# Gate weights split anew in every block of a streaming conformer layer, instead of stored split

## The chip, the cores and the metric

The kernel runs on one core of a Trainium2 chip. The metric is the time of one execution on the device, in microseconds (us). The engines are TensorE (PE in the profile; its weight loads are PEld), VectorE (DVE), ScalarE (ACT), GpSimd (POOL) and SyncE (SP), which here only issues transfers between HBM and SBUF. Each engine works through its own instructions in order and waits on semaphores for the others.

## The reference

One layer of a hybrid streaming encoder over 2048 prompt tokens and 64 sample tokens, with 1024 channels. The parts that matter:

```
h = rms_norm(x) * (1 + sc1) + sh1
z = h @ w_in                      # 1024 x 4608
glu_a, glu_b, q, k, v, g_conv, g_attn = split(z)   # 512 x5, 1024 x2
u = glu_a * sigmoid(glu_b)
conv_out = silu(layer_norm(depthwise31(u))) @ w_conv_out
attn_out = band_attention(q, k, v) @ w_attn_out    # 8 heads of 64
merged = sigmoid(g_conv) * conv_out + sigmoid(g_attn) * attn_out
x = x + gt1 * (merged @ w_o)
x = x + gt2 * swiglu_ffn(rms_norm(x) ...)
```

All of it is float32. The two gates are 2048 of the 4608 columns of `w_in`; their weights are what the change is about.

## The kernel before, in words

**Precision.** TensorE multiplies in fp32r. To keep float32 accuracy, every operand is split in two: `hi` is the value copied to fp32r, `lo` is the value minus `hi`. A product is three matmuls, hi by hi, hi by lo and lo by hi (`mm3`). So each weight slab exists as a pair `whi`, `wlo`: ScalarE makes `whi` by a copy, and `wlo` is a subtraction on VectorE or GpSimd.

**Two parts.** Part one (to about 1192 us) works through four blocks of tokens (576, 512, 512, 512). In each block come the stages q, glu0, k, glu1, v, glu2, glu3 and g, the gates. The gates of a block are 16 columns of 128 channels; their weights are 16 slabs of 128 partitions x 1024 numbers (512 KB), two for a pair of columns. Beside these matmuls of TensorE run, as lanes that a planner interleaves: the attention heads, the depthwise convolution (31 taps for each of four channel groups, on VectorE, `y<-u,wd,y`), its layer norm (`conv_norm`: sums on GpSimd in tile `s`, means by matmul in `pm`), the norm of the next block's tokens (`norm_tile`: load `x_t`, transpose into `pt`), and the conditioning products. Part one leaves the convolution's result in `c_d`, attention's in `o_d` and the gates in `g_d`, all in HBM. Part two merges them with the gates (`merge`, from `cin` and `tg`), and does the output projection and the feed-forward.

**Weights.** The class `Weights` holds a list of keys in order of use. At its making, it decides which occurrence of a key is loaded raw (an `item`: staged in `wst`, three buffers, then split) and which is taken from a split copy in HBM: a key that `kept` names and that comes again is loaded raw once; `split` then writes `whi` and `wlo` to HBM (`w_d...`), and later occurrences load the pair from there, ready for use. A key ("in", column, h) of three elements is a gate slab; a key ("in", column) of two is a slab of the GLU. `whi` and `wlo` each have five buffers. In `split`, `on_dve` says where the low part is computed.

**What sets the order.** `Stream` and `Lane` form a planner: each instruction that is written adds an estimate to its engine's load, and a lane takes its next step when the step's due time is reached by TensorE's load and when the named engines are not too far ahead of it. Transfers are issued at due times in the same way. So an estimate added to ScalarE or GpSimd moves what is written after it. The result is written to each engine's queue, and the queue is in order.

**End of part one.** The convolution's norm of block 3 ends with four groups `ln`, each split into `part_h` (ScalarE) and `part_l` and stored to `c_d`; the last heads end with the same kind of pair, stored to `o_d`. There are two buffers of each. Then part two's pools take the place of part one's, and the first tiles there wait for the last users of that space.

Of the kernel before, what the change touches and what calls it, by code (L numbers as in the profile page):

```python
# [263 lines left out]
class Weights:  # L264
# [5 lines left out]
    def __init__(self, engines, pool, dram, stream, keys, source, staging, held, kept):  # L270
        self.stream = stream
        self.sync, self.act, self.dve, self.gps = engines
        self.pool, self.dram, self.keys, self.source = pool, dram, keys, source

        self.staging, self.held, self.reach = staging, held, 0
        self.sum_pool, self.sum_d, self.sums, self.hold, self.landed = None, None, {}, 0, {}
        self.behind = nullcontext

        self.room, self.leaving = {"wst": 1, "wup": 0, "wfo": 0}, {"wst": 0, "wup": 0, "wfo": 0}
        times, raws = {}, {}  # L280
        self.items, self.users, self.need, self.first, self.stored, self.spread = [], [], {}, set(), {}, set()

        def item(key):
            self.items.append(key)
            self.users.append(0)
            return len(self.items) - 1

        for i, key in enumerate(keys):
            n = times[key] = times.get(key, 0) + 1
            if key[0] == "up" and n == 1:  # L290
                self.first.add(i)
                cs = [c for f, op in key[1:] for c in self.columns_of(f, op)]
                for c in cs:
                    if c not in raws:
                        raws[c] = item(("fi", c))
                self.need[i] = sorted({raws[c] for c in cs})
                for f, op in key[1:]:
                    for c in self.parts_of(f, op):
                        self.users[raws[c]] += 1
            elif key[0] == "dn":  # L300
                fs = [key[:3], (*key[:2], key[2] + 1)]
                for f in fs:
                    if f not in raws:
                        raws[f] = item(("fo", f[2]))
                self.need[i] = [raws[f] for f in fs]
                for op in key[3:]:
                    for e in self.rows_of(op):
                        self.users[raws[fs[e]]] += 1
            elif n == 1 or not kept(key) or n == 2 and key[:2] == ("qkv", 0):
                self.need[i] = [item(key)]  # L310
                self.users[self.need[i][0]] += 1
                if key[0] == "fo" and key[1] in last_rows(0) and n == 1:
                    self.spread.add(self.need[i][0])
        self.raws = raws
# [136 lines left out]
    def split(self):  # L451
        i = len(self.ready)
        key = self.keys[i]
        its = self.need.get(i, ())
        if key[0] == "dn":
            shape = [P, len(key) - 3, 512]
        elif i in self.first:
            shape = [P, 4 * len(key) - 4, P]
        else:
            shape = list(self.loaded[its[0]][0].shape) if its else self.stored[key][1]  # L460
        hi = self.pool.tile(shape, F32R, tag="whi", name="whi", bufs=self.held)
        lo = self.pool.tile(shape, F32R, tag="wlo", name="wlo", bufs=self.held)
        self.ready.append((hi, lo))
        if not its:
            for t, d in zip((hi, lo), self.stored[key][0]):
                self.sync.dma_start(t.bitcast(F32), d)
            return
        turn = {"wo": key[1], "fi": key[1] // P if key[0] == "fi" else 0}.get(key[0], 0)

        passing = key[:2] == ("qkv", 0) and i < 4  # L470
        on_dve = key[0] == "in" or key[0] == "qkv" and (passing or key[1]) or turn % 2
        if key[0] == "dn":
            parts = [(slice(j, j + 1), self.second(key, op)) for j, op in enumerate(key[3:])]
            self.stream.after("act", "pool")
        elif i in self.first:
            parts = [(slice(4 * j, 4 * j + 4), self.operand(f, op)) for j, (f, op) in enumerate(key[1:])]
            self.stream.after("act", "pool")
        else:
            n = 4 if key[0] == "fi" else shape[1]
            parts = [(slice(j, j + n), self.loaded[its[0]][0][:, j : j + n]) for j in range(0, shape[1], n)]  # L480
        for c, src in parts:

            late = key[0] in ("up", "fo") and self.stream.load["pool"] - self.stream.load["pe"] > POOL_BEHIND
            e, name = (self.dve, "dve") if on_dve or late else (self.gps, "pool")
            self.act.activation(hi[:, c], src, AF.Copy)
            self.stream.after(name, "act")
            e.tensor_tensor(lo[:, c], src, hi[:, c].bitcast(F32), ALU.subtract)
        if i in self.first:
            its = [self.raws[c] for f, op in key[1:] if op[0] == "a" for c in self.parts_of(f, op)]
        if key[0] == "dn":  # L490
            its = [self.raws[*key[:2], key[2] + int(op[1]) - 1] for op in key[3:] if op[0] == "b"]
        for j in its:
            self.drop(j, name)
        if key[0] == "dn" and key[3] == "b11":
            self.sum_second(key)

        def then():
            if key in self.again and key not in self.stored and not passing:
                ds = [self.dram.tile(shape, F32, name="w_d" + "_".join(map(str, key)) + "_" + part) for part in "hl"]
                for t, d in zip((hi, lo), ds):  # L500
                    self.sync.dma_start(d, t.bitcast(F32))
                self.stored[key] = ds, shape
            self.presum()

        self.stream.at(self.stream.when(name), then, True)
# [67 lines left out]


DOWN_OPERANDS = (("b11", "b21"), ("t3", "t2"), ("t1", "t4"), ("b22",))


def mod_order():
# [33 lines left out]
def streaming_layer(ctx: ExitStack, tc: tile.TileContext, I, O):  # L612
    nc = tc.nc
# [973 lines left out]
    M.fill()  # L1587
    next(vectors_)
    xs = first_rows()
    W = Weights((nc.sync, act, dve, gps), wpool, dram, stream, list(weight_order()), source, 3, 5, lambda key: key[0] in KEPT)  # L1590
    first_block(xs)
    norm_lane.add(cached_kv())
    mods = mod_steps()
# [661 lines left out]
```

## Time and profile before

| | us |
|---|---|
| runs | 2988.55, 2989.11, 2995.56 |
| median | 2989.11 |
| span of the profiled execution | 2982.2 |
| part one, start to first `cin` matmul | 1192.3 |
| TensorE busy | 2906.6 (97%) |
| VectorE busy | 2047.4 (69%) |
| ScalarE busy | 1363.6 (46%) |
| GpSimd busy | 1165.8 (39%) |

The profiled execution gives only its span; the runs' times also have what lies around it, so the two stand side by side, 6.9 us apart for the median.

Rows of the profile read: engine, operation, output<-inputs by the program's names, shape, count | busy us, mean ns of one | idle time of the engine just before them, and what ended most of it. A row of waits reads: engine and output, the releaser, then us in total, times, longest. A row of the timeline reads: start, duration, engine, line, operation, and in brackets the idle time before it with its releaser. Nearly all compute has line L102, a helper; tiles tell the operations apart. A window row lists each engine's busy us in that stretch with its count, then TensorE's granted clock, the DMA engines' busy share and GB/s.

### The profile page before, as it was taken

Reading aid. Unit: us, or ns where it says so; the run is one execution under the profiler, and the core shown is the slowest. Engines: PE = TensorE matmul, PEld = TensorE weight load, DVE = VectorE, ACT = ScalarE, POOL = GpSimd, SP = SyncE. Lnnn points to the kernel's source line nnn. Section 1 sums busy time; section 2 is a strip of 40 time slices with the busy share of each in tenths; the row PEclk is TensorE's granted clock in tenths of the full one; section 3 lists DMA queues with packets and bytes.
Section 4 is the critical chain, followed back from the end, with each engine's and each line's share of the span. In section 5 each row is a group of like instructions: output and inputs, shape, how many; then the busy total and the mean of one; then the engine's idle time right before and its main releaser. Section 6 shows DMA issues by size and latency. Waiting matters only on the chain. (4 is left out here: it accounts for less than half of the span.)

```text
span 2982.2 us, 44930 instructions
## 1 busy us (share of the span) xinstructions
PE 2906.6 (97%) x16241; PEld 2588.0 (87%) x16241; DVE 2047.4 (69%) x3628; ACT 1363.6 (46%) x2459; POOL 1165.8 (39%) x752
## 2 busy tenths in 40 slices
PE   7999899999999999989999999999999999999999
PEld 4899777787888888878989899999999999999998
DVE  5897687667857885477677755676666557566666
ACT  3345643662456257464443335544444345444442
POOL 0201310111011102444666443365766742465767
PEclk9999999999999999999999999999999999999999
DMA  8989889888997888885444786423333975333333
GB/s 296 304 282 306 264 286 312 279 256 276 308 283 221 281 256 277 265 284 167 139 147 149 233 268 222 135 89 113 114 106 116 308 244 184 98 96 114 114 104 126
DMA packets 467724, 628.06 MB, mean 211 GB/s; under 512 B 36276, under 2 KB 314664, under 8 KB 467501
## 3 DMA queue, kind: packets, MB, share of 16 engines
q1 hardware_dynamic: 453456, 605.58, 62.8%
q10 hardware_dynamic: 14045, 19.60, 1.9%
q8 instruction: 128, 2.10, 0.3%
q14 instruction: 95, 0.78, 0.1%
HBM read 476.53 MB, written 148.54 MB: 210 GB/s over the span
## 5 line engine op out<-in xcount | busy, mean ns | idle before, releaser
L102 PE MATMUL ps<-t,whi 128*128 128x384 f32 (+1 forms) x2112 | 502.7, 322 | 9.5 <-ACT t L102 4.9
L102 POOL TENSOR_TENSOR wlo<-wst,whi 128x1024 fp32r<-128x1024 f32 (+1 forms) x160 | 365.1, 2292 | 254.1 <-ACT whi L102 231.9
L102 ACT ACTIVATE whi<-wst 128x1024 fp32r<-128x1024 f32 (+1 forms) x264 | 257.4, 977 | 324.8 <-PE ps L102 118.5
L102 PE MATMUL ps<-b,whi 128*128 128x384 f32 (+1 forms) x1584 | 381.3, 326 | 6.1 <-DVE early L102 3.4
L102 PEld LDWEIGHTS ps<-t,whi 128*128 128x128 f32 x2112 | 367.6, 188 | 17.2 <-ACT t L102 5.1
L102 DVE SCALAR_TENSOR_TENSOR y<-u,wd,y 128x512 f32<-128x512 f32 (+1 forms) x480 | 369.1, 773 | 6.4
L102 PE MATMUL ps<-hh,whi 128*128 128x512 f32 (+2 forms) x992 | 361.3, 364 | 0.0
L102 DVE TENSOR_TENSOR acc<-acc,pd 128x512 f32<-128x512 f32 (+1 forms) x482 | 322.5, 685 | 54.9 <-PE pd L102 52.4
L102 PE MATMUL ps<-hl,whi 128*128 128x512 f32 (+2 forms) x992 | 345.2, 348 | 0.0
L102 PE MATMUL ps<-hh,wlo 128*128 128x512 f32 (+2 forms) x992 | 344.9, 348 | 0.0
L102 PE MATMUL ps<-t,wlo 128*128 128x384 f32 (+1 forms) x1056 | 339.3, 321 | 1.0 <-POOL wlo L102 0.7
L102 PE MATMUL pd<-whi,hid 128*128 128x512 f32 (+1 forms) x956 | 307.2, 391 | 0.2 <-DVE hid L102 0.2
L102 PEld LDWEIGHTS ps<-b,whi 128*128 128x128 f32 x1584 | 278.6, 189 | 12.4 <-DVE early L102 4.2
L102 POOL TENSOR_TENSOR r<-t,mhalf 128x1 f32<-128x1 f32 (+3 forms) x68 | 83.7, 1232 | 456.4 <-DVE t L102 451.3
L102 PE MATMUL ps<-b,wlo 128*128 128x384 f32 (+1 forms) x792 | 256.9, 325 | 0.0
L102 ACT ACTIVATE pr<-pr,sm 128x640 f32<-128x640 f32 (+3 forms) x272 | 200.2, 747 | 109.7 <-DVE sm L102 107.1
L102 PEld LDWEIGHTS pd<-whi,hid 128*128 128x128 f32 (+1 forms) x956 | 174.6, 183 | 42.4 <-ACT hid L102 0.7
L102 PEld LDWEIGHTS ps<-hh,wlo 128*128 128x128 f32 x992 | 186.6, 188 | 21.7
L102 PEld LDWEIGHTS ps<-hh,whi 128*128 128x128 f32 x992 | 187.2, 189 | 18.5 <-issue 1.6
L102 PEld LDWEIGHTS ps<-hl,whi 128*128 128x128 f32 x992 | 187.3, 189 | 15.5 <-issue 1.4
L102 PEld LDWEIGHTS ps<-t,wlo 128*128 128x128 f32 x1056 | 198.2, 188 | 2.6 <-POOL wlo L102 1.3
L102 POOL TENSOR_TENSOR wlo<-ws,whi 128x512 fp32r<-128x512 f32 x96 | 125.2, 1325 | 173.7 <-ACT whi L102 170.8
(227 smaller groups left out, 6307.0 us busy)
## 6 DMA issues: line engine op xcount, KB each, us to landing
whi<-w_din_h SPq DMA_DIRECT2D x72, 512.0 KB, 6.6
wlo<-w_din_l SPq DMA_DIRECT2D x72, 512.0 KB, 8.2
wst<-sum_d SPq DMA_DIRECT2D x132, 256.0 KB, 2.8
wfo<-in_w_ffn_out SPq DMA_DIRECT2D x64, 512.0 KB, 3.3
wmod<-in_w_ada SPq DMA_DIRECT2D x46, 512.0 KB, 6.2
sum_d<-ws SPq DMA_DIRECT2D x88, 256.0 KB, 2.4
wst<-in_w_ffn_in SPq DMA_DIRECT2D x84, 256.0 KB, 3.1
wst<-in_w_in SPq DMA_DIRECT2D x40, 512.0 KB, 9.1
```

The lines of the kernel that those rows point to most:

```text
L102: self.last = f(*args, **kw)
```

## The change

Gate slabs are taken out of `kept`. They are no longer written split; each block loads them raw into `wst` and splits them. The first occurrence has its low part on VectorE as before, every later one (set `anew`) on GpSimd.

```
--- before.py
+++ after.py
@@ -279,6 +279,7 @@
         self.room, self.leaving = {"wst": 1, "wup": 0, "wfo": 0}, {"wst": 0, "wup": 0, "wfo": 0}
         times, raws = {}, {}
         self.items, self.users, self.need, self.first, self.stored, self.spread = [], [], {}, set(), {}, set()
+        self.anew = set()
 
         def item(key):
             self.items.append(key)
@@ -287,6 +288,8 @@
 
         for i, key in enumerate(keys):
             n = times[key] = times.get(key, 0) + 1
+            if n > 1 and gate_slab(key):
+                self.anew.add(i)
             if key[0] == "up" and n == 1:
                 self.first.add(i)
                 cs = [c for f, op in key[1:] for c in self.columns_of(f, op)]
@@ -468,7 +471,7 @@
         turn = {"wo": key[1], "fi": key[1] // P if key[0] == "fi" else 0}.get(key[0], 0)
 
         passing = key[:2] == ("qkv", 0) and i < 4
-        on_dve = key[0] == "in" or key[0] == "qkv" and (passing or key[1]) or turn % 2
+        on_dve = key[0] == "in" and i not in self.anew or key[0] == "qkv" and (passing or key[1]) or turn % 2
         if key[0] == "dn":
             parts = [(slice(j, j + 1), self.second(key, op)) for j, op in enumerate(key[3:])]
             self.stream.after("act", "pool")
@@ -573,6 +576,11 @@
 
 
 DOWN_OPERANDS = (("b11", "b21"), ("t3", "t2"), ("t1", "t4"), ("b22",))
+
+
+def gate_slab(key):
+
+    return key[0] == "in" and len(key) == 3
 
 
 def mod_order():
@@ -1587,7 +1595,7 @@
     M.fill()
     next(vectors_)
     xs = first_rows()
-    W = Weights((nc.sync, act, dve, gps), wpool, dram, stream, list(weight_order()), source, 3, 5, lambda key: key[0] in KEPT)
+    W = Weights((nc.sync, act, dve, gps), wpool, dram, stream, list(weight_order()), source, 3, 5, lambda key: key[0] in KEPT and not gate_slab(key))
     first_block(xs)
     norm_lane.add(cached_kv())
     mods = mod_steps()
```

In numbers: block 0 loses 32 stores of 512 KB; blocks 1 to 3 load 48 raw slabs where they loaded 48 pairs; ScalarE gets 48 copies, GpSimd 48 subtractions. The matmuls stay.

The rows below show each engine's queue as built, in order, one instruction a row. In them `hist` and `u` copies are the convolution's history of 30 tokens, `s` is its norm's sum, `y` the convolution's result; numbers behind names tell buffers of the program apart, and a bracket lists the semaphores waited for. First GpSimd, in block 1's gates; before, between the three sums of the taps' results:

```order
L102 COPY hist_181<-u_4777 128x30 [waits DVE_49]
L102 TENSOR_TENSOR s_5905<-y_4271 128x512 [waits DVE_49]
L102 COPY u_7286<-hist_181 128x30 [waits Pool_49]
L102 COPY hist_181<-u_5175 128x30 [waits DVE_49]
L102 COPY hist_181<-u_5297 128x30 [waits DVE_49]
L102 TENSOR_TENSOR s_5905<-s_5905,y_4271 128x512 [waits DVE_49,Pool_49]
L102 COPY u_7691<-hist_181 128x30 [waits Pool_49]
L102 TENSOR_TENSOR s_5905<-s_5905,y_4271 128x512 [waits DVE_49,Pool_49]
L102 COPY u_7987<-hist_181 128x30
```

and after, from the first sum to the last split ahead of the second:

```order
L102 TENSOR_TENSOR s_5968<-y_4204 128x512 [waits DVE_49]
L102 COPY u_7120<-hist_181 128x30 [waits Pool_49]
L102 TENSOR_TENSOR wlo_5115<-wst_3637,whi_5114 128x1024 [waits DMAHW5_49,DMAHW2_49,DMAHW6_49,DMAHW1_49,DMAHW7_49,PE_49,Activation_49]
L102 TENSOR_TENSOR wlo_5159<-wst_3680,whi_5158 128x1024 [waits DMAHW4_49,DMAHW3_49,DMAHW7_49,PE_49,Activation_49]
L102 COPY hist_181<-u_5108 128x30 [waits DVE_49]
L102 TENSOR_TENSOR wlo_5241<-wst_3869,whi_5240 128x1024 [waits DMAHW1_49,DMAHW7_49,PE_49,Activation_49]
L102 TENSOR_TENSOR wlo_5340<-wst_5144,whi_5339 128x1024 [waits DMAHW2_49,DMAHW5_49,PE_49,Activation_49]
L102 TENSOR_TENSOR wlo_5442<-wst_5183,whi_5441 128x1024 [waits DMAHW4_49,DMAHW6_49,PE_49,Activation_49]
L102 COPY hist_181<-u_5234 128x30 [waits DVE_49]
L102 TENSOR_TENSOR wlo_5592<-wst_5300,whi_5591 128x1024 [waits DMAHW2_49,PE_49,Activation_49]
L102 TENSOR_TENSOR wlo_5596<-wst_5389,whi_5595 128x1024 [waits DMAHW3_49,PE_49,Activation_49]
L102 TENSOR_TENSOR wlo_5758<-wst_5479,whi_5757 128x1024 [waits DMAHW1_49,PE_49,Activation_49]
```

Eight splits of gate slabs now stand between the first sum and the next, and three more between that and the last sum, on an engine that had only copies there.

Second, SyncE's queue at the end of part one. Before, the four convolution pairs (`c_d`) are out ahead of the last attention pair (`o_d`), and the first gate load of part two follows:

```order
L1311 DMA c_d_67<-part_h_12317 128x512 [waits DMAHW7_49,Activation_49]
L1311 DMA c_d_67<-part_l_12318 128x512 [waits DMAHW0_49,DVE_49]
L375 DMA wst_12408<-in_w_conv_out 128x4x128 [waits DMAHW1_49,Pool_49]
L375 DMA wst_12408<-in_w_attn_out 128x4x128 [waits DMAHW2_49]
L1311 DMA c_d_67<-part_h_12414 128x512 [waits DMAHW3_49,Activation_49]
L1311 DMA c_d_67<-part_l_12415 128x512 [waits DMAHW4_49,DVE_49]
L375 DMA wst_12641<-in_w_o 128x1024 [waits DMAHW6_49,Pool_49]
L375 DMA wst_12684<-in_w_o 128x1024 [waits DMAHW7_49,DMAHW5_49,Pool_49]
L891 DMA gt_d_70<-row_12479 32x128 [waits DMAHW1_49,DVE_49]
L1417 DMA o_d_66<-part_h_12547 128x512 [waits DMAHW2_49,Activation_49]
L1417 DMA o_d_66<-part_l_12548 128x512 [waits DMAHW3_49,DVE_49]
L1108 DMA tg_12562<-g_d_68 128x320 [waits DMAHW3_49,DMAHW2_49,DMAHW4_49,DMAHW1_49,DMAHW5_49,DMAHW0_49,PE_49]
```

After, the last attention pair comes first and four convolution pairs follow; the first gate load of part two waits for more of them:

```order
L1425 DMA o_d_66<-part_l_12536 128x512 [waits DMAHW3_49,DVE_49]
L1319 DMA c_d_67<-part_h_12547 128x512 [waits DMAHW4_49,Activation_49]
L1319 DMA c_d_67<-part_l_12548 128x512 [waits DMAHW5_49,DVE_49]
L1319 DMA c_d_67<-part_h_12555 128x512 [waits DMAHW6_49,Activation_49]
L378 DMA wst_12805<-in_w_o 128x1024 [waits DMAHW7_49,Pool_49]
L1319 DMA c_d_67<-part_l_12556 128x512 [waits DMAHW0_49,DVE_49]
L1319 DMA c_d_67<-part_h_12563 128x512 [waits DMAHW1_49,Activation_49]
L1319 DMA c_d_67<-part_l_12564 128x512 [waits DMAHW2_49,DVE_49]
L1319 DMA c_d_67<-part_h_12571 128x512 [waits DMAHW3_49,Activation_49]
L1116 DMA tg_12645<-g_d_68 128x320 [waits DMAHW4_49]
L1319 DMA c_d_67<-part_l_12572 128x512 [waits DMAHW5_49,DVE_49]
L1116 DMA tg_12594<-g_d_68 128x320 [waits DMAHW3_49,DMAHW2_49,DMAHW5_49,DMAHW1_49,DMAHW6_49,DMAHW0_49,PE_49]
```

The convolution's stores have moved behind the heads' last one, next to the start of part two.

Third, SyncE's queue ahead of block 1, at the loads of its token tiles. Before:

```order
L501 DMA w_din_4352_0_h_3194<-whi_3128 128x1024 [waits DMAHW1_49]
L501 DMA w_din_4352_0_l_3195<-wlo_3129 128x1024 [waits DMAHW2_49]
L1311 DMA c_d_67<-part_h_3267 128x64 [waits DMAHW4_49,Activation_49]
L1311 DMA c_d_67<-part_l_3268 128x64 [waits DMAHW5_49,DVE_49]
L1121 DMA x_t_3330<-in_x_prompt 128x1024 [waits DMAHW6_49]
L1121 DMA x_t_3332<-in_x_prompt 128x1024 [waits DMAHW0_49]
L1121 DMA x_t_3334<-in_x_prompt 128x1024 [waits DMAHW1_49]
```

After:

```order
L378 DMA wst_2122<-in_w_in 128x4x256 [waits DMAHW5_49,DVE_49]
L1438 DMA bias_194<-rb_d_71 64x576 [waits DMAHW6_49,DVE_49]
L1129 DMA x_t_3270<-in_x_prompt 128x1024 [waits DMAHW7_49]
L1129 DMA x_t_3272<-in_x_prompt 128x1024 [waits DMAHW1_49]
L1129 DMA x_t_3274<-in_x_prompt 128x1024 [waits DMAHW2_49]
L1401 DMA vv_2316<-v_d_65 128x2x128 [waits DMAHW4_49,PE_49]
L1403 DMA vv_2316<-v_d_65 64x128 [waits DMAHW5_49]
L378 DMA wst_2314<-in_w_in 128x4x256 [waits DMAHW6_49,DVE_49]
```

The first three token tiles (`x_t`) stand at rows 231 to 233 of this queue before and at 152 to 154 now. The fourth stands, before and after, right behind the two stores of the pair `w_dqkv_0_2`, at rows 277 and 243.

More of the change, by code (lines that the diff above doesn't have):

```diff
@@ L281, in __init__ @@
         self.items, self.users, self.need, self.first, self.stored, self.spread = [], [], {}, set(), {}, set()
+        self.anew = set()
         def item(key):
@@ L289, in __init__ @@
             n = times[key] = times.get(key, 0) + 1
+            if n > 1 and gate_slab(key):
+                self.anew.add(i)
             if key[0] == "up" and n == 1:
@@ L470, in split @@
         passing = key[:2] == ("qkv", 0) and i < 4
-        on_dve = key[0] == "in" or key[0] == "qkv" and (passing or key[1]) or turn % 2
+        on_dve = key[0] == "in" and i not in self.anew or key[0] == "qkv" and (passing or key[1]) or turn % 2
         if key[0] == "dn":
@@ L575, with gate_slab @@
 DOWN_OPERANDS = (("b11", "b21"), ("t3", "t2"), ("t1", "t4"), ("b22",))
+def gate_slab(key):
+    return key[0] == "in" and len(key) == 3
 def mod_order():
@@ L1589, in streaming_layer @@
     xs = first_rows()
-    W = Weights((nc.sync, act, dve, gps), wpool, dram, stream, list(weight_order()), source, 3, 5, lambda key: key[0] in KEPT)
+    W = Weights((nc.sync, act, dve, gps), wpool, dram, stream, list(weight_order()), source, 3, 5, lambda key: key[0] in KEPT and not gate_slab(key))
     first_block(xs)
```

## The prediction

> **What bounds the kernel now.** I read the page's first part, then the windows of part one, then the waits of TensorE there, then the groups and the timeline around the places that the change touches.
>
> ```profile
> span 2982.2 us, 44930 instructions
> PE 2906.6 (97%) x16241; PEld 2588.0 (87%) x16241; DVE 2047.4 (69%) x3628; ACT 1363.6 (46%) x2459; POOL 1165.8 (39%) x752
> ...
> whi<-w_din_h SPq DMA_DIRECT2D x72, 512.0 KB, 6.6
> wlo<-w_din_l SPq DMA_DIRECT2D x72, 512.0 KB, 8.2
> ...
> wst<-in_w_in SPq DMA_DIRECT2D x40, 512.0 KB, 9.1
> ```
>
> TensorE is busy 97% of the span. The change leaves its matmuls as they are, so the time moves only where TensorE's waits or its clock move. By stage of part one (length, then busy time per engine, clock, DMA share, GB/s):
>
> ```profile
> core 0: us, PE busy (x) PEld busy (x) DVE busy (x) ACT busy (x) POOL busy (x), PEclk, DMA share, GB/s
> 350.00:375.00 25.00, 22.14 (x99) 17.67 (x100) 20.53 (x49) 14.63 (x28) 8.35 (x5) 0.86 0.78 243
> 332.00:496.00 164.00, 151.76 (x811) 119.14 (x813) 116.80 (x252) 65.54 (x146) 26.36 (x21) 0.98 0.91 296
> 496.00:632.00 136.00, 132.38 (x749) 112.59 (x742) 98.40 (x196) 76.57 (x142) 13.38 (x14) 1.00 0.91 287
> 1046.00:1187.00 141.00, 140.28 (x748) 118.99 (x746) 103.44 (x200) 92.01 (x160) 23.05 (x15) 1.00 0.87 271
> ```
>
> The first row is the start of block 1, the next is that block ahead of its gates, the third its gates, the last the gates of block 3. The DMA share is about 0.9 in all of them, yet TensorE is idle for 3.6 us of 136 and 0.7 of 141. What it waits for in the whole of part one:
>
> ```profile
> PE pt L102 <- DVE x_t L102: 11.8, 7, 5.7
> PE sc L102 <- DVE sm L102: 7.3, 7, 2.3
> ...
> PE ps L102 <- DMA whi<-w_dqkv_h: 1.1, 1, 1.1
> PE ps L102 <- DMA wlo<-w_dqkv_l: 0.8, 2, 0.5
> ```
>
> Weights that arrive late cost 1.9 us, and none of them is a gate slab. The large entry is the norm of new token rows (pt, from x_t), most of it at the start of block 1; the next is attention's scores, which wait for VectorE's maxima.
>
> **Transfers removed.** Block 0 no longer writes 16 slabs as hi and lo (32 writes of 512 KB, 16 MB), and blocks 1 to 3 load 48 slabs of 512 KB where they loaded 96: 40 MB fewer of 628. Since TensorE never waits for a gate slab, their cover is TensorE's own work and the saving is worth 0 by itself. Two places may feel less traffic. First, the 1.1 + 0.8 us on w_dqkv: between 0 and −1.9; I take −1. Second, the start of block 1:
>
> ```profile
> w_din_h<-whi SPq DMA_DIRECT2D x24, 512.0 KB, 5.6
> w_din_l<-wlo SPq DMA_DIRECT2D x24, 512.0 KB, 6.4
> ...
> 338.92 1.11 SPq L1121 DMA_DIRECT2D x_t<-in_x_prompt  x1
> ```
>
> The fourth token tile is issued at 338.92 and TensorE's transposes wait for it, 5.7 us at the longest; in the 25 us behind, the clock was 0.86, a loss of 25 × 0.14 = 3.5 us. All x_t waits and that loss make 11.8 + 3.5 = 15.3 us, of which I count at most 13 as reachable here, because some of the seven waits are at the first block's start. The order puts the first three token tiles far earlier in SP's queue, but the fourth stays behind the two writes of the same qkv slab and behind its own waits for TensorE. So between −13 and 0; I take −4, nearer to nothing, because the longest wait is that of the tile which keeps its place.
>
> **Splits added.** Each of 48 slabs needs an ACT copy and, on GpSimd, a subtraction. Block 0's stay on VectorE, so VectorE gains and loses nothing directly.
>
> ```profile
> L102 POOL TENSOR_TENSOR wlo<-wst,whi 128x1024 fp32r<-128x1024 f32 x9 | 22.4, 2489 | 50.6 <-ACT whi L102 39.1 <-PE po L102 9.5 <-PE ptp L102 1.0
> L102 ACT ACTIVATE whi<-wst 128x1024 fp32r<-128x1024 f32 x45 | 47.5, 1058 | 43.3 <-PE ps L102 24.5 <-DMA wst<-in_w_in 8.9 <-DMA gqk<-in_k_norm_g 4.3
> L102 DVE SCALAR_TENSOR_TENSOR y<-u,wd,y 128x512 f32<-128x512 f32 x360 | 268.2, 749 | 5.4
> ```
>
> ACT: 48 × 1.058 = 51 us, 17 per block, into gate stages where it has 59 and 49 us idle (136 − 76.57, 141 − 92.01). Hidden, 0; with that cover gone it would cost up to 17 a block. GpSimd: 48 × 2.49 = 119 us, 40 per block, where it is busy 13 and 23 us of some 140. By room it is hidden. By order it stands in line with the convolution's sums, which wait for VectorE's taps:
>
> ```profile
> 463.15 1.10 POOL L102 TENSOR_TENSOR s<-y 128x512 f32<-128x512 f32 x1 [28.76 <-DVE y L102]
> ...
> 548.47 1.09 POOL L102 TENSOR_TENSOR s<-s,y 128x512 f32<-128x512 f32 x1 [24.97 <-DVE y L102]
> ```
>
> A split queued behind such a sum waits with it. In the order, the first split behind each sum is needed by TensorE 130 rows or more after the scores that stand ahead of the last tap, some 25 us at the pace of these stages (749 matmuls in 136 us). So no wait from that, 0.
>
> What is not hidden is the meeting with the taps. Between the first and the last of these sums stand 11, 11 and 15 of a block's 16 splits, 37 in all, beside VectorE's taps; before, nothing stood there but copies of 30 columns. How a GpSimd instruction meets VectorE ones that read two SBUF tiles:
>
> ```profile
> 792.60 1.29 POOL L102 TENSOR_TENSOR s<-s,y 128x512 f32<-128x512 f32 x1 [15.05 <-DVE y L102]
> ...
> 793.18 2.04 DVE L102 SCALAR_TENSOR_TENSOR y<-u,wd,y 128x512 f32<-128x512 f32 x2
> ...
> 1352.74 2.41 POOL L102 TENSOR_TENSOR wlo<-wfo,whi 128x1024 fp32r<-128x1024 f32 x1 [6.77 <-ACT whi L102]
> ...
> 1353.22 2.48 DVE L102 TENSOR_TENSOR wlo<-ws,whi 128x512 fp32r<-128x512 f32 x1 [1.08 <-ACT whi L102]
> ```
>
> Two taps of 0.749 took 2.04, and the second VectorE instruction lasted until just after GpSimd's ended. VectorE loses up to 2.4 us per split, 1.2 if the two meet at random. TensorE feels it where scores come next:
>
> ```profile
> 1177.45 0.81 DVE L102 CUSTOM_DVE_ANT_0 pr<-sc,bias 128x640 f32<-128x640 f32 x1
> ...
> 1178.90 0.74 PE L102 MATMUL sc<-kk,q 128*128 128x320 f32 x4
> ```
>
> Here 0.64 us lay between the end of the maximum and the next scores. A meeting of 1.2 less 0.64 is 0.56, and I count every second split as standing ahead of a maximum: 37 × 0.28 = 10 us. The bounds are 0 (VectorE idles 38 us in each such stage) and 37 × 2.43 = 90. I take +10, nearer to 0, since 7 waits of this kind cost only 7.3 us so far.
>
> The Trainium skill, "SBUF — State Buffer", section "🔬 SBUF: two separate sides", says that VectorE and GpSimd share a port pair by an exclusive lock, held for the whole instruction by whichever starts first. The rows above agree (2.48 for an instruction beside 2.41 on GpSimd); by that rule taken at its full length for each split, the term would be the 90 us end instead of 10.
>
> **Order moved at the end of part one.** With ACT and GpSimd fuller, the planner writes the last convolution's norm later: its second mean stands 66 TensorE rows before part two's first matmul, where it stood 267. All four of its stores (c_d) now stand behind the last head's (o_d), and the gate load of part two that follows waits for all of them.
>
> ```profile
> 1168.22 0.34 SPq L1311 DMA_DIRECT2D c_d<-part_h  x1
> ...
> 1174.75 0.63 ACT L102 ACTIVATE part_h<-ln 128x512 fp32r<-128x512 f32 x1 [3.35 <-DMA c_d<-part_h]
> ...
> 1192.30 0.56 PE L102 MATMUL ps<-cin,whi 128*128 128x320 f32 x2 [1.40 <-DVE o_p L102]
> ...
> 1193.66 1.00 SPq L1417 DMA_DIRECT2D o_d<-part_l  x1
> 1196.60 0.80 SPq L1108 DMA_DIRECT2D tg<-g_d  x2
> ```
>
> Part two starts at T = 1192.30; its first o_d store goes out 0.6 later. There are two part buffers, so three landings follow in series, each 2.9 us (1193.66 to 1196.60) to 6.5 (1168.22 to 1174.75), plus about 1.4 for copy, low part and issue: the last lands at T + 0.6 + 3 × 4.3 = T + 13.5, or T + 0.6 + 3 × 7.9 = T + 24.3. The split of the first merged column waits for that, and until it is done TensorE can fill four banks: two columns of 24 matmuls, 3.5 us each, 7.0 in all. The wait is 13.5 + 0.5 − 7.0 = 7 to 24.3 + 0.5 − 7.0 = 18; I take the middle, +12.
>
> **Sum.** −1 − 4 + 10 + 12 = +17 against the profiled execution: 2982.2 + 17 = 2999.2. What lies around the span is 2989.11 − 2982.2 = 6.9, with the median of the runs taken for this execution's own time: 3006. A difference of 0.3% (9 us) is about what a measurement of this kernel can tell from no change.
>
> **Rivals.** *Faster:* the x_t waits at block 1 vanish (−13), and both the tail and the meetings stay in VectorE's idle time: −13 − 1, 2975. It decides at one point: the fourth token tile must be there before TensorE reaches its transposes, that is some 6 us earlier. For it speaks that 16 MB of writes leave the queue; against it that the tile keeps its place in the order. *Only the tail:* meetings cost nothing, 3006 − 10 = 2996, within 0.3%. For it speak 38 us of VectorE idle per stage. *VectorE becomes the bound of the gate stages:* with half of the 90 us reaching TensorE instead of 10, 3006 + 35 = 3041. A split of 2.43 every 8.5 us of a gate stage (136 / 16) adds at most 39 us to VectorE's 98 of 136: full to the last microsecond. The rule of the Trainium skill named above, at full length, points this way. Against it: GpSimd too can be the one that waits, and it is not urgent. *The change does not act:* the order shows 48 new splits, so no.
>
> **How the numbers follow.** Main case (2999 to 3025) 0.58, only the tail 0.20, faster 0.10, VectorE as bound 0.12. The likeliest gives 3006. The range leaves out most of the fast case and of the slow one: 2986 (below the second rival by 10, if the tail costs 7 and block 1 gives up to 9) to 3032 (tail 18 and meetings of 30 in place of 12 and 10). Slower by over 0.3%: 0.58 + 0.12 = 0.70, less 0.02 for main cases that end just below 2998: 0.68. Within: 0.22. Faster: 0.10.
>
> **What the changed profile would show.** For the meetings: in the gate stages, a mean of VectorE's taps above 749 ns, and the wait of sc for sm above 7.3 us. For the tail: a gap of TensorE of 7 to 18 us some 7 us after the first cin matmul, put down to VectorE or ACT behind a store of c_d. For block 1: the x_t wait at 7 to 8 instead of 11.8, the clock after it above 0.86. For the transfers: 48 fewer loads of gate slabs, a lower DMA share in the gate stages, and no TensorE wait for wst. The forecast is wrong if a wait of ps for wlo on GpSimd appears in the gate stages (the queue does stall the splits), or if the gap at the transition is missing.

## The result and the profile after

The changed kernel is slower by 1%: 3020.97 us median (3016.79 to 3027.49) against 2988.83 (2982.78 to 2995.56), a ratio of 1.0104 with a 95% interval of 1.0084 to 1.0125. That is 32 us. The profiled execution spans 3021.7, against 2982.2 before, so the two traces stand 39.5 apart: that of the changed kernel took 3023.48, 2.5 above its median, and that of before was a quick one. The 6.9 us between its span and the median are mostly that: in the runs that list both, the time is 1.8 us above the span (3023.48 − 3021.7), so it took some 2984, 5 under the median. From the page of the kernel after:

```profile
span 3021.7 us, 44983 instructions
...
PE 2920.7 (97%) x16241; PEld 2599.8 (86%) x16241; DVE 2089.4 (69%) x3627; ACT 1411.6 (47%) x2507; POOL 1291.3 (43%) x801
...
HBM read 451.36 MB, written 131.76 MB: 193 GB/s over the span
```

HBM moves 42 MB less (476.53 read and 148.54 written before). TensorE has the same 16241 matmuls and is busy 14 us longer: part of them ran at a lower clock. VectorE is busy 42 us longer, although it lost and gained no instruction of weight. By stage, the rows of the three gate stages of the kernel after (blocks 1, 2 and 3):

```profile
core 0: us, PE busy (x) PEld busy (x) DVE busy (x) ACT busy (x) POOL busy (x), PEclk, DMA share, GB/s
...
489.30:625.90 136.60, 127.73 (x683) 108.93 (x683) 103.49 (x180) 78.96 (x137) 41.58 (x26) 0.98 0.66 204
...
777.90:915.40 137.50, 129.64 (x717) 109.84 (x716) 105.30 (x180) 79.91 (x138) 44.23 (x26) 0.98 0.62 190
...
1064.20:1213.70 149.50, 140.64 (x731) 118.04 (x730) 106.50 (x185) 95.31 (x159) 45.38 (x23) 0.99 0.64 184
```

The DMA share fell from about 0.9 to 0.66 and less, GpSimd's busy time rose to over 40 us, and TensorE is idle 8 to 9 us in each, with a clock just below full. Where the time appears is seen best by following the same matmul through the two traces. The table takes the n-th of the 992 matmuls `ps<-hh,wlo`, which come in the same sequence in all kernels here, and the first `pw` of part two, and gives how much later than before it starts (us, profiled executions; the rows below the first belong to the experiments). Within a stage the difference also shows attention moved past these matmuls, so the ends of long stretches count, not single steps. A few us of each entry are scatter between executions: e3_pass, e7_half and e11_pass_two have the instructions of before, but for one memset, up to their first added one, at 473 us or later, and at 470 us they already stand 0.7, 3.2 and 2.5 us behind it.

| kernel | block 1, end of its front (497.7) | end of its gates (630.8) | block 2, end of front (775.4) | end of gates (906.7) | block 3, end of front (1046.1) | end of gates (1184.0) | first `pw` (1216.4) |
|---|---|---|---|---|---|---|---|
| after | −8.4 | −4.9 | 2.5 | 8.7 | 18.1 | 29.7 | 38.2 |
| e1_dve | −11.4 | −20.5 | −10.2 | −16.4 | −8.8 | −0.7 | 13.8 |
| e2_lows | −3.8 | −11.2 | −5.3 | −8.0 | −3.5 | 0.0 | 7.5 |
| e3_pass | 2.4 | 13.1 | 12.9 | 21.8 | 27.3 | 37.3 | 38.3 |
| e4_untold | −7.3 | 9.6 | 9.8 | 30.9 | 34.0 | 47.6 | 47.5 |
| e5_writes | 1.2 | 3.9 | 12.4 | 18.6 | 25.2 | 36.5 | 44.7 |
| e6_lows_untold | −4.9 | −5.8 | −5.9 | −5.6 | −5.0 | −5.0 | −5.1 |
| e7_half | 3.9 | 5.2 | 5.4 | 7.0 | 10.1 | 12.3 | 12.5 |

For the kernel after, three parts: 8 us gained at the start of block 1, 38 lost from there to the end of block 3's gates (−8.4 to 29.7), and some 9 lost at the start of part two. These add up to the distance of the two traces at that point, 38.2, and the medians stand only 32 apart, so the middle part is some 30 to 38. What TensorE waits for, kernel after, over the whole span:

```profile
PE sc L102 <- DVE sm L102: 16.7, 13, 4.0
PE ps L102 <- DVE t L102: 10.2, 2, 9.8
PE po L102 <- DVE pl L102: 8.6, 8, 4.0
PE ptp L102 <- ACT pr L102: 7.7, 7, 3.3
...
PE pt L102 <- DVE x_t L102: 4.2, 4, 1.4
```

The norm's wait fell from 11.8 to 4.2. Attention's three links with VectorE and ScalarE rose: `sc` from 7.3 to 16.7, `po` and `ptp` from 0 and 1.4 to 8.6 and 7.7. Before:

```profile
PE ptp L102 <- ACT pr L102: 1.4, 3, 0.7
```

One entry is new, 9.8 us at the start of part two. The taps are the group of VectorE that grew (part one, kernel after; 268.2 us and 749 ns before):

```profile
L102 DVE SCALAR_TENSOR_TENSOR y<-u,wd,y 128x512 f32<-128x512 f32 x360 | 306.0, 853 | 4.7
```

The 360 taps take 37.8 us more. Read instruction by instruction, 22 of the 48 gate splits run at the same time as a tap, 1.7 us of delay each; the other 26 lie beside other work of VectorE or none. One place shows how this reaches TensorE. The timeline of block 1's gates, kernel after, a row each of VectorE, GpSimd, VectorE and TensorE:

```profile
517.92 5.48 DVE L102 SCALAR_TENSOR_TENSOR y<-u,wd,y 128x512 f32<-128x512 f32 x5
...
520.47 2.38 POOL L102 TENSOR_TENSOR wlo<-wst,whi 128x1024 fp32r<-128x1024 f32 x1 [12.68 <-ACT whi L102]
...
523.33 0.68 DVE L102 TENSOR_TENSOR pl<-ptp,ph 128x512 fp32r<-128x512 f32 x1
...
524.06 0.58 PE L102 MATMUL po<-pl,vv 128*128 128x256 f32 x1 [4.00 <-DVE pl L102]
```

Five taps last 5.48 us where five of 0.749 make 3.75. The split on GpSimd lies within them. Behind the taps stands `pl`, attention's low part, and TensorE waits 4.00 us for it. Then the clock falls (windows of the kernel after, around that wait):

```profile
core 0: us, PE busy (x) PEld busy (x) DVE busy (x) ACT busy (x) POOL busy (x), PEclk, DMA share, GB/s
520.00:524.00 4.00, 0.06 (x1) 0.00 (x0) 4.00 (x4) 0.40 (x1) 2.38 (x1) 0.90 0.01 1
524.00:530.00 6.00, 5.94 (x19) 5.27 (x20) 4.43 (x8) 2.77 (x4) 4.03 (x3) 0.50 0.53 177
530.00:536.00 6.00, 6.00 (x29) 5.03 (x28) 5.91 (x12) 2.87 (x6) 0.71 (x1) 1.00 0.80 247
```

TensorE is busy for 5.94 us of the middle row at a clock of 0.50 and does 19 matmuls where the next row does 29. A wait of 4 us costs some 3 us more behind it. Summed over all such stretches between 300 and 1260 us (TensorE's busy time in them, times the missing share of the clock), the kernel before loses 2.9 us in one stretch, the kernel after 18.1 in seven. Four of the seven, 9.2 us, lie in the part where the 38 us are lost (489.3 to 1213.7 in this trace, 497.7 to 1184.0 before). In that part TensorE is idle 25 us longer than before, 22.5 of it by the waits of `sc`, `po` and `ptp` in the rows above, and busy 13 us longer.

At the start of part two (T = 1220.77 in this trace), rows of TensorE and VectorE of the kernel after:

```profile
1220.77 0.56 PE L102 MATMUL ps<-cin,whi 128*128 128x320 f32 x2 [1.40 <-DVE o_p L102]
...
1234.15 0.69 DVE L102 TENSOR_TENSOR part_l<-ln,part_h 128x512 fp32r<-128x512 f32 x1 [3.18 <-DMA c_d<-part_l]
...
1237.35 0.49 DVE L102 SCALAR_TENSOR_TENSOR t<-tg,ps 128x320 f32<-128x320 f32 x1 [2.51 <-DMA c_d<-part_l]
...
1237.90 0.90 PE L102 MATMUL ps<-cin,whi 128*128 128x320 f32 x2 [9.83 <-DVE t L102]
```

The last low part of the convolution waits for a buffer whose store has to land, its own store lands 16.6 us behind T (1237.35 − 1220.77), and only then does VectorE take up the merge that frees TensorE's banks.

### The profile page after: what moved, and what is told of

Same layout as the page of the kernel before. It is cut to its first block, busy times and chain, and to the rows that moved or that the text cites. A ratio compares the mean times of both kernels' runs of the same rounds, so it can differ in the third digit from the quotient of the medians.

```text
span 3021.7 us, 44983 instructions
## 1 busy us (share of the span) xinstructions
PE 2920.7 (97%) x16241; PEld 2599.8 (86%) x16241; DVE 2089.4 (69%) x3627; ACT 1411.6 (47%) x2507; POOL 1291.3 (43%) x801
## 4 chain that ended last, share of the span: by engine, by line
PE 50%; DVE 3%; DMA 1%; ACT 1%; issue 1%; POOL 1%; SPq 0%; ACTq 0%; POOLq 0%; DVEq 0%
PE ps L102 29%; PE pd L102 15%; PE pw L102 5%; DVE wlo L102 1%; ACT whi L102 1%; DVE pw L102 0%; POOL wlo L102 0%; POOL ws L102 0%; DVE t L102 0%; DVE ps L102 0%; DMA cin<-o_d 0%; DMA x<-x_d 0%; PE pt L102 0%; DMA wst<-in_w_ffn_in 0%; DMA wup<-in_w_ffn_in 0%
## 5 line engine op out<-in xcount | busy, mean ns | idle before, releaser
L102 POOL TENSOR_TENSOR wlo<-wst,whi 128x1024 fp32r<-128x1024 f32 (+1 forms) x212 | 492.9, 2335 | 445.9 <-ACT whi L102 427.3
L102 ACT ACTIVATE whi<-wst 128x1024 fp32r<-128x1024 f32 (+1 forms) x311 | 307.6, 992 | 345.5 <-PE ps L102 125.8
L102 DVE SCALAR_TENSOR_TENSOR y<-u,wd,y 128x512 f32<-128x512 f32 (+1 forms) x480 | 407.4, 851 | 5.7
L102 PEld LDWEIGHTS ps<-b,whi 128*128 128x128 f32 x1584 | 279.2, 190 | 12.9 <-DVE early L102 4.2
```

What stands on the lines that cost most here:

```text
L102: self.last = f(*args, **kw)
```

## Experiments

**The theory** after the traces: GpSimd's subtractions and VectorE's taps get in each other's way; the taps' delay goes on to attention's maxima and low parts, TensorE waits and its clock falls. The moved order makes the wait at part two. **The rival:** ScalarE's 48 copies, the raw loads or the moved order delay attention, whoever subtracts.

**e1_dve: the low parts on VectorE in all blocks.**

```
-        on_dve = key[0] == "in" and i not in self.anew or key[0] == "qkv" and (passing or key[1]) or turn % 2
+        on_dve = key[0] == "in" or key[0] == "qkv" and (passing or key[1]) or turn % 2
```

> One condition put back: the low parts of all gate slabs are subtracted on VectorE, in every block. Theory of the port (GpSimd's splits block VectorE's taps, TensorE then waits for attention and its clock halves): the taps are back at a mean of 750 to 760 ns from 851, VectorE gets 48 x 1.21 = 58 us of subtractions, some 19 us per gate stage that had 38 us idle, so the waits in blocks 1 to 3 go back to about those of before, and the time is 2985 to 3000. Rival (ScalarE's 48 copies and the raw loads are what delays attention, whoever subtracts): within 6 us of the changed kernel, 3015 to 3027.

Measured: 2996.3 us, ratio 1.0024 (1.0014 to 1.0034). Taps of e1_dve in part one:

```profile
L102 DVE SCALAR_TENSOR_TENSOR y<-u,wd,y 128x512 f32<-128x512 f32 x360 | 269.2, 750 | 4.4
```

The planner counts these subtractions on VectorE, so the order differs too. With 48 more subtractions of its own, VectorE's taps are as quick as before, and the kernel is 25 us faster than the one with GpSimd's. The rival falls for the larger part. By the table it is ahead of the kernel before up to the end of block 2's gates and in block 3 gives back 15.7 (−16.4 to −0.7), then 14.5 at part two; its part-one waits there are spread over `kk` loads, a late weight stage and `pl`, and were not followed further.

**e2_lows: the changed kernel with its order and copies, without GpSimd's work.** Block 0 stores the low parts; later blocks load raw slab and low part. `stream.add` gives the planner the estimate without an instruction.

```
+            if i in self.anew:
+                self.stream.add("pool", "tensor_tensor", 1024, (), {})
+                self.sync.dma_start(lo.bitcast(F32), self.lows[key])
+            else:
                 e.tensor_tensor(lo[:, c], src, hi[:, c].bitcast(F32), ALU.subtract)
...
         def then():
+            if gate_slab(key) and i not in self.anew:
+                self.lows[key] = self.dram.tile(shape, F32, name="w_d" + "_".join(map(str, key)) + "_l")
+                self.sync.dma_start(self.lows[key], lo.bitcast(F32))
```

> The changed kernel with its order and its ScalarE copies, and the planner told of the same GpSimd work, but GpSimd does none: block 0 stores the low parts alone (8 MB) and blocks 1 to 3 load raw slab and low part. Theory of the port: taps at 750 ns, the +33 us of blocks 1 to 3 gone but for a few, the wait at the start of part two (9.8 us) still there, the gain of 8 us at block 1's start halved by the stores: 2989 + 9 - 4 = about 2994, 2988 to 3002. Rival (copies, order): 3012 to 3027.

Measured: 2988.37 us, ratio 1.0003 (0.9993 to 1.0012). Its taps, and the waits of TensorE in its stretch 1180 to 1240:

```profile
L102 DVE SCALAR_TENSOR_TENSOR y<-u,wd,y 128x512 f32<-128x512 f32 x360 | 268.8, 750 | 4.7
```

```profile
PE ps L102 <- DVE t L102: 9.3, 2, 8.5
```

By the table it stands at 0.0 where the changed kernel stands at 29.7, and loses 7.5 to the first `pw`. Copies, raw loads and order are all in it: they do not make the loss of blocks 1 to 3, and they do make that of part two.

**e3_pass: the kernel before, with nothing but GpSimd's work added.** Each stored low part, once loaded, has zero subtracted in place; the planner is not told, so that the order of the rest stays.

```
                 self.sync.dma_start(t.bitcast(F32), d)
+            if key[0] == "in" and len(key) == 3:
+                self.gps.engine.tensor_tensor(lo, lo.bitcast(F32), self.zero.unsqueeze(2).to_broadcast(shape), ALU.subtract)
             return
...
```

> The kernel before, with its order, its stored pairs and no added copy; GpSimd alone gets 48 instructions of 128x1024 that the planner is not told of: once a stored low part has landed, it subtracts zero from it in place. Theory of the port: 2989 + 25 to 35 (the rise of blocks 1 to 3 in the changed kernel, 33 us, without its gain at block 1 and without its loss at part two's start): 3010 to 3025, taps above 830 ns. Rival (copies, order, raw loads): 2986 to 2995.

Measured: 3022.8 us, ratio 1.0111 (1.0096 to 1.0127). Its groups in part one, and its waits of TensorE between 325 and 1260:

```profile
L468 POOL TENSOR_TENSOR wlo<-wlo,zero 128x1024 fp32r<-128x1024 f32 x48 | 94.8, 1978 | 148.8 <-DMA wlo<-w_din_l 115.9 <-PE ps L102 17.4 <-DVE sm L102 9.5
...
L102 DVE SCALAR_TENSOR_TENSOR y<-u,wd,y 128x512 f32<-128x512 f32 x360 | 295.9, 827 | 5.4
```

```profile
PE sc L102 <- DVE sm L102: 21.1, 16, 3.0
```

GpSimd's instructions alone, in the order of before, cost 34 us. With e2_lows this settles the cause of the loss in blocks 1 to 3. The size here need not be that of bare subtractions: the pass works in place, so TensorE may use the slab only after it. No wait of TensorE is put down to the pass in this trace.

**e4_untold: the changed kernel, the planner not told of copies and splits.**

```
+            if i in self.anew:
+                self.act.engine.activation(hi[:, c], src, AF.Copy)
+                self.gps.engine.tensor_tensor(lo[:, c], src, hi[:, c].bitcast(F32), ALU.subtract)
+                continue
```

> The changed kernel, but the planner is not told of the 48 copies and 48 subtractions, so that the convolution's norm stands where it stood before: its second mean 267 rows ahead of part two, not 66. Theory of the port, with the order as the cause of the wait at part two's start only: that wait of 9.8 us and the low clock after it are gone, the rise of blocks 1 to 3 stays: 3021 - 10 = 3011, 3003 to 3016. Rival (the moved order is the cause of both): 2980 to 2995.

Measured: 3030.38 us, ratio 1.0138 (1.0123 to 1.0153): a miss, by 19 us. Its taps in part one, and its waits of TensorE between 1215 and 1275:

```profile
L102 DVE SCALAR_TENSOR_TENSOR y<-u,wd,y 128x512 f32<-128x512 f32 x360 | 311.5, 869 | 5.2
```

```profile
PE ps L102 <- DVE o_p L102: 1.4, 1, 1.4
PE ptp L102 <- ACT pr L102: 0.6, 1, 0.6
PE ps L102 <- DVE t L102: 0.5, 1, 0.5
```

The wait at part two is gone, as expected: the moved order was its cause (by the table, 47.6 to 47.5). But blocks 1 to 3 lose 55 (−7.3 to 47.6) instead of 38. So the planner's knowledge of the splits was worth 17 us there and cost 9 at part two; how much of the 17 is the order on VectorE and how much that on ScalarE was not separated.

**e5_writes: the changed kernel, block 0's stores put back**, read by nothing.

```
-            if key in self.again and key not in self.stored and not passing:
+            if (key in self.again or gate_slab(key) and i not in self.anew) and key not in self.stored and not passing:
```

> The changed kernel, with the 32 stores of block 0's split gate slabs put back (16 MB, read by nothing). If the stores are what made block 1's token tiles late, the 8 us gained by the end of block 1's front are lost again: 3021 + 8 = 3029, 3025 to 3033. If the gain comes from the token tiles' earlier place in SyncE's queue, which stays: 3017 to 3024.

Measured: 3032.57 us, ratio 1.0144 (1.0128 to 1.0159), 11.6 above the changed kernel. Its wait for the token tiles between 325 and 1260, the same as that of before:

```profile
PE pt L102 <- DVE x_t L102: 6.9, 2, 5.7
```

By the table, the end of block 1's front goes from −8.4 to 1.2. The expectation took the tiles' earlier place to stay. It did not: with the stores, the planner puts the first three tiles back to rows 231 to 233. Only the fourth, whose wait is the 5.7 us, keeps the same transfers ahead of it but for the 32 stores. Its issue, in the kernel after and in e5_writes (338.92 before):

```profile
320.13 0.52 SPq L1129 DMA_DIRECT2D x_t<-in_x_prompt  x1
...
339.20 0.83 SPq L1129 DMA_DIRECT2D x_t<-in_x_prompt  x1
```

So the stores cost the gain, and the fourth tile goes out 19 us later with them. Whether they do it as rows of the queue or as traffic, and what the first three tiles' place is worth, these runs do not separate.

**e6_lows_untold: e2_lows, with the planner told of neither copies nor splits.**

```
-            self.act.activation(hi[:, c], src, AF.Copy)
-            self.stream.after(name, "act")
             if i in self.anew:
-                self.stream.add("pool", "tensor_tensor", 1024, (), {})
+                self.act.engine.activation(hi[:, c], src, AF.Copy)
                 self.sync.dma_start(lo.bitcast(F32), self.lows[key])
```

> As the run that stores low parts alone (no split on GpSimd, 48 copies on ScalarE), but the planner is told of neither copies nor splits, so that the convolution's norm keeps its place of before. If the moved order is what costs 10 us at part two's start, and the copies are hidden: 2988 - 10 = 2978, 2974 to 2984, faster than before. If ScalarE's copies are not hidden once the planner leaves no room for them: 2988 to 3000.

Measured: 2979.72 us (2978.17 to 2982.56), ratio 0.9965 (0.9952 to 0.9977): faster than both kernels. Its copies and taps, over 325 to 1260 and over part one:

```profile
L489 ACT ACTIVATE whi<-wst 128x1024 fp32r<-128x1024 f32 x48 | 50.4, 1052 | 23.6 <-PE ps L102 23.5
```

```profile
L102 DVE SCALAR_TENSOR_TENSOR y<-u,wd,y 128x512 f32<-128x512 f32 x360 | 268.2, 749 | 5.2
```

50 us of copies on ScalarE are hidden even where nothing was planned for them, the loss at part two is gone, and with half of block 0's stores left, 5 us of the gain at block 1 remain to the end (by the table; by the medians this kernel is 10.6 us ahead, because the trace of before is a quick one).

**e7_half: e3_pass with half-sized passes.**

```
-                self.gps.engine.tensor_tensor(lo, lo.bitcast(F32), self.zero.unsqueeze(2).to_broadcast(shape), ALU.subtract)
+                half = lo[:, : shape[1] // 2]
+                self.gps.engine.tensor_tensor(half, half.bitcast(F32), self.zero.unsqueeze(2).to_broadcast([P, shape[1] // 2, shape[2]]), ALU.subtract)
```

> As the run that adds 48 passes of GpSimd to the kernel before (3022.8), with each pass over half the columns: 128x512, about 1.25 us. If each meeting costs in proportion to GpSimd's time: 2989 + 17 = 3006, 3002 to 3010. If a slack of about 0.6 us ahead of attention's maxima has to be used up first, and stalls too short to halve the clock cost only themselves: less than half, 2992 to 3001.

Measured: 2998.44 us, ratio 1.0030 (1.0017 to 1.0042): 8.2 us for 48 instructions of 1.12 us, where those of 1.98 cost 34. The time is that of the second expectation, but its slack is not the reason: the taps below lost only 7.4 us to begin with.

```profile
L469 POOL TENSOR_TENSOR wlo<-wlo,zero 128x512 fp32r<-128x512 f32 x48 | 53.6, 1118 | 175.6 <-DMA wlo<-w_din_l 144.3 <-PE ps L102 14.7 <-issue 6.4
...
L102 DVE SCALAR_TENSOR_TENSOR y<-u,wd,y 128x512 f32<-128x512 f32 x360 | 275.6, 770 | 5.4
```

**e10_two and e11_pass_two: the same work of GpSimd in instructions half as long**, in the changed kernel and in e3_pass. The edit of e10_two; e11_pass_two cuts the pass of e3_pass in the same way.

```
+            cut = [slice(0, 128), slice(128, 256)] if i in self.anew else [slice(0, None)]
+            for w in cut:
+                e.tensor_tensor(lo[:, c, w], src[:, :, w], hi[:, c, w].bitcast(F32), ALU.subtract)
```

> The changed kernel with each of its 48 GpSimd subtractions cut into two of half the columns (128x4x128), one behind the other: GpSimd's total stays about 119 us, the longest time for which one instruction can hold VectorE halves. If the length of one GpSimd instruction decides: blocks 1 to 3 rise by 15 to 22 instead of 38, 2996 to 3008. If the total time of GpSimd beside the taps decides: 3017 to 3027.

> The kernel before with 48 passes of GpSimd, each now cut into two instructions of 128x512: all the GpSimd time of the full passes (3022.8) in pieces as long as those of the half passes (2998.4). If the length of one instruction decides: 2989 + 2 x 9 = 3007 or less. If the total decides: 3018 to 3027.

Measured: e10_two 3016.16 us, ratio 1.0085 (1.0060 to 1.0110); e11_pass_two 3012.07, ratio 1.0075 (1.0054 to 1.0097). Both lie between or beside the two expectations. GpSimd's instructions and the taps in part one, first of e10_two, then of e11_pass_two:

```profile
L102 POOL TENSOR_TENSOR wlo<-wst,whi 128x512 fp32r<-128x512 f32 x96 | 135.4, 1435 | 185.3 <-ACT whi L102 172.2 <-PE sc L102 9.8 <-DMA whi<-w_din_h 3.2
...
L102 DVE SCALAR_TENSOR_TENSOR y<-u,wd,y 128x512 f32<-128x512 f32 x360 | 301.2, 840 | 4.7
```

```profile
L470 POOL TENSOR_TENSOR wlo<-wlo,zero 128x512 fp32r<-128x512 f32 x96 | 113.3, 1203 | 137.4 <-DMA wlo<-w_din_l 127.8 <-PE ptp L102 4.0 <-PE sc L102 3.1
...
L102 DVE SCALAR_TENSOR_TENSOR y<-u,wd,y 128x512 f32<-128x512 f32 x360 | 286.7, 801 | 5.4
```

GpSimd's total did not stay the same: it is 113.3 us where e3_pass has 94.8. Even so, cutting takes a third off what e3_pass loses (22.5 us for 33.8). In the changed kernel it takes 4.8 us off, which the spread of the runs does not tell from nothing. In the kernels that have the order of before, what the taps lose and what the kernel loses go together: 7.4 and 8.2 us in e7_half, 18.5 and 22.5 in e11_pass_two, 27.7 and 33.8 in e3_pass. The kernel loses what the taps lose and a tenth to a fifth more. That is a sum of waits and of half clock, as in the kernel after, and no sign that each microsecond of the taps is passed on.

**e9_norm9: the kernel before, token tiles asked for two gate columns earlier.**

```
-NORM_G = 11
+NORM_G = 9
```

> The kernel before, with one number changed: the next block's token tiles are asked for after gate column 9 instead of 11. If block 1's wait for x_t and the low clock after it are a matter of when the tiles are issued: 2989 - 8 = 2981, 2976 to 2985. If the fourth tile, which waits for its buffer, sets that wait: 2986 to 2992.

Measured: 2990.84 us, ratio 1.0003 (0.9993 to 1.0013). Waits between 325 and 1260:

```profile
PE sc L102 <- DVE sm L102: 6.2, 7, 1.7
...
PE pt L102 <- DVE x_t L102: 3.1, 1, 3.1
PE ptp L102 <- ACT pr L102: 3.1, 2, 2.5
```

The wait for the tiles fell from 6.9 to 3.1, and nothing came of it: the earlier norm moved other work, `ptp` waits appeared, and the clock was low for 23.9 us in three stretches (9.9 us lost, by the sum used above) where it had been for 6.8 in one. So this run does not test either expectation cleanly.

## Why the prediction was right, and where it was off

The forecast was 3006, slower; measured were 3020.97. The direction and the range held. The rise is 32 where 17 was forecast, so one term was too small. That the range held is in part luck: its upper end allows the meetings 30 us, they cost 30 to 38, and the gain at block 1 and a tail below its forecast made up for it.

- **Transfers removed, 0 by themselves.** Right: no wait for a gate slab was there to gain, and DMA's share fell (0.66, 0.62 and 0.64 in the three gate stages) without a gain there.
- **Start of block 1, −4 (0 to −13).** It was −8, within the bounds, and the reason for leaning towards nothing was wrong. The fourth tile kept its place relative to its neighbours, but with 32 stores fewer ahead of it it was issued 19 us earlier. The bound of −13 was too far: only two of the seven waits, 6.9 us, are at block 1. The sign named for the clock failed: in the kernel after it is halved there for 10.2 us (from 338.9), where it had been for 6.8 (from 351.9).
- **ScalarE's copies, 0.** Right: e2_lows carries all of them at no cost, e6_lows_untold too.
- **Splits queued behind the convolution's sums, 0.** Right: TensorE waits for GpSimd's `wlo` 0.7 us in the whole span, as before.
- **The meeting of splits and taps, +10 (0 to 90).** The mechanism was right, the size was not: +38 between the traces, 34 in e3_pass. The step that failed is "I count every second split as standing ahead of a maximum: 37 × 0.28". The loss of the taps before that step, 37 × 1.2 = 44, is near the 37.8 measured, by luck: 22 splits met a tap, at 1.7 us each. The step took 34 of the 44 off again, and the runs do not: e7_half, e11_pass_two and e3_pass lose more than the taps do. Slack took off some: TensorE's three waits behind the taps rose by 22.5 us. But the 0.64 ahead of the scores was used for every link, while `pl` and the probabilities behind the taps are late too (8.6 and 7.7 us of wait). And the clock was counted at block 1 but not here: stretches at half clock give 9.2 us back. The five taps at 517.92 suggest why VectorE's 38 us of idle time per stage were the wrong place to look: it worked through a row that does not pause when attention needs it.
- **Late weights of qkv, −1.** The entries on `w_dqkv` (1.9 us in all) are gone from TensorE's waits, within the bounds; e6_lows_untold still has one of 1.8. Loads of `kk` are late instead, 4.0 us in four waits, which the forecast did not have and no run explains.
- **The end of part one, +12 (7 to 18).** The wait is 9.8, the last landing T + 16.6 (forecast: T + 13.5 to T + 24.3), the loss 8 to 10. That the planner's order was the cause, e4_untold and e6_lows_untold show by its absence, and e2_lows, which keeps the order and the wait.
- **The rivals.** The faster case had its condition met, the tile came in time, and was undone by the other two terms. VectorE as the bound (3041, half of the 90 us) comes nearer in its term, 45 against a measured 30 to 38 where the main case had 10, and lies 20 us above the result where the main case lies 15 below. Its mechanism did not come: VectorE is busy 76% of block 1's gates (103.49 of 136.60 us), not full; its work is late, not too much. The rule of the Trainium skill, "SBUF — State Buffer", section "🔬 SBUF: two separate sides", points at the right pair of engines; the traces agree that the two hold one another up (5.48 us for five taps; the 22 splits that meet a tap last 2.57 us on average, the others mostly 2.40), and e3_pass and e2_lows that GpSimd's work is the cause; that a port is what they share, no run here shows. At its full length for every split it gives 90; the taps lost 37.8.

## What to carry to other kernels

A subtraction that fits into GpSimd's idle time is not free while VectorE works on SBUF operands: price it by what VectorE loses (here 1.7 us for each split of 2.4 that meets a tap, 0.8 over all 48). If VectorE is in the chain between two of TensorE's matmuls, take that loss as the estimate of what the kernel loses, half clock included. A wait of TensorE of a few microseconds has a second price behind it, 1.7 us or more at half the clock here (half of a stretch of 3.4), so a sum of waits is too low. And where a planner's estimates set the order, take apart what the instructions cost and what the planner does about them: here, telling it nothing and having no GpSimd work gave the only version faster than the kernel before (0.9965).

## What was not expected of the hardware

GpSimd's instructions cost VectorE out of proportion to their length: 48 of 1.12 us took 7.4 us from the taps (0.15 each), 96 of 1.20 took 18.5 (0.19 each), 48 of 1.98 took 27.7 (0.58 each). Counted one by one, half or nearly half of them meet a tap in each kernel (21 of 48, 48 of 96, 24 of 48), and what grows is the price of a meeting: 0.35, 0.39 and 1.15 us. With the 1.7 of the splits and the 0.77 of e10_two's halves, it is in all five traces the undisturbed length of the GpSimd instruction (1.04, 1.04, 1.89, 2.40, 1.29) less 0.5 to 0.75 us. Not every instruction of VectorE is held: `pl`, which reads one of its inputs from PSUM, takes within a split what it takes elsewhere. From the kernel after:

```profile
1053.93 2.40 POOL L102 TENSOR_TENSOR wlo<-wst,whi 128x1024 fp32r<-128x1024 f32 x1 [4.80 <-ACT whi L102]
...
1055.61 0.69 DVE L102 TENSOR_TENSOR pl<-ptp,ph 128x512 fp32r<-128x512 f32 x1 [0.55 <-ACT ph L102]
```

The low clock came in stretches of 3.4 us or two to four times that in all these traces, and short waits were enough. Windows of the kernel after around a wait of 1.99 us for `kk`:

```profile
core 0: us, PE busy (x) PEld busy (x) DVE busy (x) ACT busy (x) POOL busy (x), PEclk, DMA share, GB/s
...
1056.20:1058.20 2.00, 0.01 (x2) 0.04 (x1) 0.10 (x1) 0.00 (x0) 0.13 (x1) 1.00 1.12 235
1058.20:1059.40 1.20, 1.20 (x8) 1.19 (x9) 0.00 (x0) 0.00 (x0) 0.00 (x0) 0.87 1.15 297
1059.40:1062.70 3.30, 3.30 (x11) 2.80 (x10) 2.54 (x5) 1.52 (x3) 0.00 (x0) 0.53 0.88 279
1062.70:1066.00 3.30, 3.30 (x21) 2.97 (x20) 2.56 (x6) 1.32 (x2) 0.00 (x0) 1.00 0.25 64
```

In the third row TensorE does 11 matmuls, in the last 21 in the same time. The Trainium skill, "TensorE: Matmul & The Clock Gate", section "🔬 Part 1: The HAM clock gate (the "warmup" mystery)", says that the clock is halved after an idle window of about 3.4 us, in windows that run freely. The lengths agree with it; the wait of 2.0 does not fill a window, and the clock fell all the same. What decides here can be counted. Cut the time from 300 to 1260 us of all twelve traces into steps of 3.41 us, in phase with the changes of the granted clock. Behind each of the 43 steps at full clock in which TensorE was busy for under 46%, the clock was halved; of 3185 that were busy for 60% or more, none; between the two, 12 of 56. The step in front of the fall at 1059.1 was 42% busy. So a wait of about 2 us, or a few short ones close together, is enough if it falls into one step.
